# A hybrid attention layer: six output tiles, the sample's sums a step later, pools that wait by tile, and a scale per token

## The chip, the cores and the metric

The kernel runs on one core of one Trainium2 chip. The metric is device time in microseconds (us) for one execution. The core has a matrix engine (PE), a vector engine (DVE), a scalar engine (ACT), a general engine (POOL) and a queue (SP) that issues all of this kernel's transfers, which 16 DMA engines carry out. Every engine takes its instructions in the order of its own queue.

## The reference

One layer of a decoder. It is computed for a prompt of 2048 tokens and for a sample of 8 sequences with 8 new tokens each, whose keys and values of the last 2048 positions lie in a cache. Cut to what matters here:

```
h = rmsnorm(x, norm_w)
q, k, v, qb, kb, vb, g_lr, gate_a, gate_b = split(h @ w_in)
q, k = rope(rmsnorm(q)), rope(rmsnorm(k))                # 8 heads x 64
o_a = mixture of 3 dilated windows (128,1) (512,4) (2048,16), weighted by their softmax denominators
o_b = gated linear attention(qb, kb, vb, g_lr, state)    # 4 heads, key 64, value 128
o_b = rmsnorm(o_b, gla_norm_w)
mixed = concat(o_a * silu(gate_a), o_b * silu(gate_b))
y = x + mixed @ w_out
```

It returns y of prompt and sample, the prompt's keys and values, the sample's new keys and values, and the states of the linear attention.

## The kernel before

Tokens go in 16 tiles of 128, called t, and the sample's 64 tokens as one tile "s". Large products use pairs of f16 tiles, a high and a low part (three products for each), and each operand is scaled by a power of two ahead of it. Intermediate results go through DRAM (q_d, k_d, o1_d to o3_d, gw_d, ga_d, ob_d and others).

The stages, in the order in which the code writes them:

1. Weights v, q and k are loaded; `first(m)` projects v, q and k for four tiles at a time (m = 0 to 3). Between its steps the main loop adds `3 * rate` to `credit` and, for every whole unit of it, advances a software pipeline of attention work by one step (`pump`). Units of branches 1 and 2 are queued after each m. A unit writes its outputs, maxima and denominators into a tile `o` of the pool `op` (L367, four tiles) and stores it to o1_d or o2_d. L414 on DVE masks the scores and takes their maxima into `o`; ACT exponentiates (L417); PE transposes (L424); ACT, and DVE or POOL, split the result into two f16 parts (L386, L387, or L389 to L391); PE multiplies by the values (L439); DVE adds two parts into `o` (L456).
2. Beside it run 64 steps of `sample_scores` (one or two after each projection of m = 2 and 3, the rest in stage 3). A step loads a row of queries (qt, L929), keys k3 (L931) and, every second time, keys k2 (L934), and calls `dot` twice: POOL multiplies into the one tile pr (L919), DVE sums it at once (L920). The tiles k3 and qt come from two buffers each, k2 and pr from one.
3. `rest("qkb")` projects the keys and queries of the linear attention, woven with what is left of the attention, with branch 3 (16 residues; its tile o3 is from the pool b3, two tiles, stored at L894), with the loading of weights g and vb (`load_w`) and with the remaining dots. `weave` runs several generators in turns: next is the one whose share of its announced number of steps is least, and one that must wait yields WAIT.
4. The attention's pools are closed; the pools gl, gt and gst take their place. g and vb are projected, woven with the linear attention (`gla_all`, GLA) and the loading of weights gb; then gb, woven with GLA and the loading of the output weights o0 and o1, until gb and the weights are done. `silu` keeps the maxima of its results by row, in one column of gmax["a"] or gmax["b"] per call.
5. The pools of the projections (wr, zp, hp, hps, on the right side of SBUF) are closed, and cb and cb1 take their place. The maxima are reduced over all columns and, by `spread_max` (a transpose on PE, a reduction, a product with ones), over all partitions. This gives one scale smx for all tokens, and from it smxa and inv_o.
6. `prompt_out`: `combine(t)` loads the three branches (L1421), ob, gw and ga (L1424 to L1428), mixes them, scales by smx and smxa, splits into two f16 parts (L1365, L1366) and transposes them by a DMA (L1368); `finish` multiplies by the output weights (L1404, 48 products a tile), rescales by inv_o and adds x (L1411), and stores y (L1415). combine runs one tile ahead. Woven with it is `sample_attention` on the pools ssk and ss1, on the left side: it loads value tiles (L1664, eight buffers) and multiplies them one step at a time (L1639).

A pool that is opened on the bytes of closed pools has all its tiles wait, by default, for every user of those pools. The engines' queues are not in the order of the code throughout: in the trace, value tiles of stage 6 are loaded while gb is still projected.

Of the kernel before, what the change touches and what calls it, by code (L numbers as in the profile page):

```python
# [18 lines left out]
P = 128  # L19
# [33 lines left out]
def tile_hymba(ctx: ExitStack, tc: tile.TileContext, A: dict):  # L53
# [293 lines left out]
    with ExitStack() as c1:  # L347
# [8 lines left out]
        def right(stack, name, bufs):  # L356
            return stack.enter_context(tc.tile_pool(name=name, bufs=bufs, side="right"))
# [9 lines left out]
        op = c_att.enter_context(tc.tile_pool(name="op", bufs=4))  # L367
# [549 lines left out]
        def dot(out, kt, qt, tag):  # L917
            pr = sk.tile([P, 512], F32, name=f"pr_{tag}", tag="pr", bufs=1)
            POOL.tensor_tensor(pr[:], kt, qt, ALU.mult)  # L919
            DVE.tensor_reduce(  # L920
                out, pr[:].rearrange("p (u k d) -> p u k d", u=2, k=4), AX.X, ALU.add
            )

        def sample_scores(b, t):
# [12 lines left out]
            dot(out[:, 1], k3[:], qt[:], f"3_{b}_{t}")  # L937
            dot(out[:, 0], sk_state["k2"][:], qt[:], f"2_{b}_{t}")
            if t == 7:
                SP.dma_start(sc_d[b * P : (b + 1) * P, :], sc[:].rearrange("p g c -> p (g c)"))  # L940
# [157 lines left out]
        for m in range(4):  # L1098
# [9 lines left out]
            rate = 0.62  # L1108
            if m == 1:
                for b in range(8):  # L1110
                    for t in (0, 4, 1, 5, 2, 6, 3, 7):
                        side.append(lambda b=b, t=t: sample_scores(b, t))
        c_first.close()
# [35 lines left out]
        gl = c_gla.enter_context(tc.tile_pool(name="gl", bufs=2))  # L1149
        gt = c_gla.enter_context(tc.tile_pool(name="gt", bufs=1))  # L1150
        gst = c_gla.enter_context(tc.tile_pool(name="gst", bufs=1))
# [83 lines left out]
        def sample_gla():  # L1235
            c_sg = ExitStack()
            g1 = c_sg.enter_context(tc.tile_pool(name="sg1", bufs=1))
# [77 lines left out]
        for names, loads, n_ in ((("g", "vb"), ("gb",), 45), (("gb",), ("o0", "o1"), 0)):  # L1315
            host = [rest(*names), sum(steps(name) for name in names)]
            fetch = [chain(*(load_w(x) for x in loads)), len(loads) * (2 * KT + 1)]
            left = weave(host, gla_all, fetch, until=[host, fetch])
            gla_all = left[0] if left else [iter(()), 1]
            gla_all[1] = n_ or 100  # L1320


        c_in.close()
        cb = right(c1, "cb", 2)
        cb1 = right(c1, "cb1", 1)
# [3 lines left out]
        bound = sm.tile([P, 2], F32, name="bound", tag="bound", bufs=1)  # L1329
        for i, n_ in enumerate("ab"):  # L1330
            g = sm.tile([P, 1], F32, name=f"gm_{n_}", tag="gm")
            DVE.tensor_reduce(g[:], gmax[n_][:], AX.X, ALU.max)
            DVE.tensor_copy(bound[:, i : i + 1], spread_max(g[:], f"g{n_}"))
        DVE.scalar_tensor_tensor(
            bound[:, 0:1], bound[:, 0:1], 2048.0, powers["v"][:], ALU.mult, ALU.mult
        )
        g = sm.tile([P, 1], F32, name="gm_n", tag="gm")
        DVE.tensor_reduce(g[:], gnw[:], AX.X, ALU.max, apply_absolute_value=True)
        DVE.scalar_tensor_tensor(
            bound[:, 1:2], bound[:, 1:2], 11.4, g[:], ALU.mult, ALU.mult  # L1340
        )
        p2 = sm.tile([P, 1], F32, name="p2", tag="p2", bufs=1)
        DVE.tensor_tensor(p2[:], bound[:, 0:1], bound[:, 1:2], ALU.max)
        power(p2[:], p2[:])
        smx = kp.tile([P, 1], F32, name="smx")
        DVE.reciprocal(smx[:], p2[:])
        DVE.tensor_scalar(smx[:], smx[:], M_SCALE, None, ALU.mult)

        smxa = kp.tile([P, 1], F32, name="smxa")
        DVE.tensor_scalar(  # L1350
            smxa[:], smx[:], powers["v"][:], 1.0 / (P_SCALE * W_SCALE * H_SCALE * V_SCALE),
            ALU.mult, ALU.mult,
        )
        inv_o = []
        for nh in range(2):
            t = kp.tile([P, 1], F32, name=f"inv_o{nh}")
            DVE.tensor_scalar(
                t[:], loaded[f"o{nh}"][1][:], p2[:], 1.0 / M_SCALE, ALU.mult, ALU.mult
            )
            inv_o.append(t)  # L1360
# [29 lines left out]
        def finish(tag, n, mixed_parts, xsrc, ydst):  # L1390
# [8 lines left out]
            for nh in range(2):  # L1399
                cs = slice(512 * nh, 512 * nh + 512)  # L1400
                w_, inv = loaded[f"o{nh}"][0], inv_o[nh]
# [15 lines left out]
        def combine(t):  # L1417
            rows = slice(t * P, (t + 1) * P)
            oc = cb.tile([P, 3, NH, 66], F32, name=f"oc_{t}", tag="oc")
            for g, src in enumerate((o1_d, o2_d, o3_d)):  # L1420
# [24 lines left out]
                w[:], w[:], smxa[:], mn[:].unsqueeze(1).to_broadcast([P, 3, NH]),  # L1445
                ALU.mult, ALU.mult,
            )
            DVE.scalar_tensor_tensor(mix[:, 512:], ob[:], smx[:], gw[:], ALU.mult, ALU.mult)
# [15 lines left out]
        def sample_out():  # L1464
# [15 lines left out]
            for i in range(2):  # L1480
                a_, b_ = ts_[2 * i : 2 * i + 2]
                DVE.scalar_tensor_tensor(
                    mix[:NS, 512 * i : 512 * i + 512], a_[:NS], smx[:NS], b_[:NS],
                    ALU.mult, ALU.mult,
                )
            yield from finish("s", NS, sample_parts(mix), x_s, y_s)

        def prompt_out():
            while 0 not in mixed:
                yield WAIT  # L1490
            mixes = {0: combine(0)}
            for t in range(NT):
                while t + 1 < NT and t + 1 not in mixed:
                    yield WAIT
                if t + 1 < NT:
                    mixes[t + 1] = combine(t + 1)
# [289 lines left out]
```

## Time and profile before

| what | us |
|---|---|
| median of 3 runs | 1474.63 (1474.44 to 1477.34) |
| the profiled execution | 1477.99 |
| its span, first to last instruction | 1476.2 |
| PE busy | 1282.4 |
| DVE busy | 980.5 |
| ACT busy | 831.8 |
| POOL busy | 622.6 |
| 16 DMA engines, mean busy share | 0.74 |

How to read the lines that the prediction shows. A line of a wait reads "engine tile line <- what ended the wait: us in total, times, longest". A line of the timeline reads "start, length, engine, line, operation, output <- inputs, shapes, count", and in square brackets the engine's idle time ahead of it and what ended it. A line of a table by windows reads "from:to length, busy us (instructions) of PE, weight load, DVE, ACT and POOL, then the granted TensorE clock, the DMA share and GB/s"; where one line or engine alone is asked for, only its columns are there. A line of the table of transfers gives the count, the size of one and the median us from issue to landing.

### The profile page before, as it was taken

What the parts mean: (1) busy time and instruction counts of PE and PEld (TensorE: products, weight loads), DVE (VectorE), ACT (ScalarE), POOL (GpSimd) and SP (SyncE); (2) the same over time, 40 slices, a digit from 0 to 9 for tenths busy, and PEclk for the clock granted to TensorE, in tenths of its full rate; (3) what the DMA queues carried; (4) which work ended last, traced back from release to release, by engine and by line L of the source; (5) the groups of instructions that cost most, each with busy time, mean ns of one, the idle gap of its engine ahead of it and who ended that gap; (6) DMA issues with size and microseconds to landing.
All of it is one profiled execution on the core that took longest, in us unless ns stands there. A gap on an engine that the chain in (4) does not pass through costs nothing. (4 is left out here: it accounts for less than half of the span.)

```text
span 1476.2 us, 25889 instructions
## 1 busy us (share of the span) xinstructions
PE 1282.4 (87%) x8628; PEld 733.9 (50%) x8628; DVE 980.5 (66%) x2393; ACT 831.8 (56%) x2263; POOL 622.6 (42%) x564
## 2 busy tenths in 40 slices
PE   4796899998989889995869999889989969999878
PEld 1343455554555555664546755667545433433323
DVE  6476687777878946665554466798887567534453
ACT  6645688676667666865657754777786621100100
POOL 0043333566766544664341376545562334212221
PEclk9998899999999899997989999989999969999989
DMA  9877668587886799879998444243135689999993
GB/s 266 262 179 182 181 176 218 152 227 218 202 212 183 224 239 277 284 207 233 268 226 203 131 127 125 93 137 115 60 115 173 201 267 292 302 318 314 288 299 122
DMA packets 321240, 306.29 MB, mean 207 GB/s; under 512 B 192258, under 2 KB 223059, under 8 KB 321107
## 3 DMA queue, kind: packets, MB, share of 16 engines
q1 hardware_dynamic: 321106, 304.64, 73.7%
q8 instruction: 68, 1.11, 0.3%
q14 instruction: 66, 0.53, 0.1%
HBM read 183.19 MB, written 79.43 MB: 178 GB/s over the span
## 5 line engine op out<-in xcount | busy, mean ns | idle before, releaser
L919 POOL TENSOR_TENSOR pr<-k,qb 128x512 f32<-128x512 f32 x128 | 173.8, 1358 | 185.2 <-DVE sck L920 88.7
L1050 PEld LDWEIGHTS <-hr 128*128 128x128 f16 x1824 | 175.8, 99 | 139.6 <-issue 19.6
L417 ACT ACTIVATE p<-p,o 128x256 f32<-128x256 f32 (+1 forms) x384 | 173.0, 453 | 93.8 <-DVE o L414 85.8
L1050 PEld LDWEIGHTS <-hl 128*128 128x128 f16 x1248 | 124.4, 102 | 148.9 <-issue 35.6
L1404 PE MATMUL Y<-w_o,mh 128*128 128x512 f16 x768 | 180.3, 388 | 17.4 <-DMA mh<-mt 12.1
L414 DVE CUSTOM_DVE_ANT_0 p<-s,m3w,scl_s 128x256 f32<-128x256 f32 (+1 forms) x384 | 143.7, 419 | 52.3 <-DMA o_d<-o 36.1
L391 POOL TENSOR_TENSOR pt<-p,pt 128x512 f16<-128x512 f32 (+1 forms) x80 | 96.3, 1204 | 156.2 <-ACT pt L390 120.6
L920 DVE TENSOR_REDUCE sck<-pr 128x8 f32<-128x512 f32 x128 | 87.0, 679 | 89.5 <-POOL pr L919 89.4
L424 PE MATMUL t<-ident,p 128*128 128x128 f32 x600 | 117.1, 292 | 30.7 <-ACT p L417 28.3
L439 PE MATMUL O<-v,pt 128*128 128x128 f16 x1200 | 115.6, 223 | 31.0 <-POOL pt L391 19.1
L1404 PEld LDWEIGHTS <-mh 128*128 128x128 f16 x768 | 73.4, 99 | 120.1 <-issue 29.4
L1050 PE MATMUL acc_v<-w_v,hl 128*128 128x512 f16 x384 | 103.7, 411 | 19.1 <-ACT zs_k L646 9.3
L406 PE MATMUL s<-kk,qq 128*128 128x256 f16 (+1 forms) x512 | 108.4, 326 | 12.6 <-DVE o L414 10.9
L439 PEld LDWEIGHTS <-pt 128*128 128x128 f16 x1200 | 85.7, 100 | 67.3 <-POOL pt L391 25.3
L1452 POOL TENSOR_TENSOR tc<-oc,w 128x512 f32<-128x512 f32 x32 | 44.2, 1400 | 158.6 <-DVE w L1444 131.6
L424 PEld LDWEIGHTS t<-ident,p 128*128 128x128 f32 x600 | 74.1, 148 | 59.2 <-ACT p L417 44.8
L1050 PE MATMUL acc_g<-w_g,hr 128*128 128x272 f16 (+1 forms) x768 | 100.1, 277 | 1.5 <-ACT vbs L720 1.5
L1050 PE MATMUL acc_q<-w_q,hl 128*128 128x512 f16 x384 | 96.3, 388 | 1.8 <-ACT zs_q L646 1.4
L1050 PE MATMUL acc_k<-w_k,hl 128*128 128x512 f16 x384 | 95.3, 383 | 0.5 <-DVE vp L733 0.5
L1050 PE MATMUL acc_vb<-w_vb,hr 128*128 128x512 f16 x384 | 90.4, 383 | 4.1 <-DVE so_g L620 4.1
L1365 ACT ACTIVATE mt<-mix 128x1024 f16<-128x1024 f32 x16 | 16.9, 1056 | 130.5 <-DVE mix L1459 100.2
L1050 PE MATMUL acc_gb<-w_gb,hr 128*128 128x512 f16 x384 | 88.7, 386 | 0.0
(529 smaller groups left out, 2588.3 us busy)
## 6 DMA issues: line engine op xcount, KB each, us to landing
k<-in_cache_k_win SPq DMA_DIRECT2D x104, 256.0 KB, 4.9
sv<-in_cache_v_win SPq DMA_DIRECT2D x104, 256.0 KB, 5.5
hr<-h_d SPq DMA_DIRECT2D x44, 512.0 KB, 4.8
qb<-q_d SPq DMA_DIRECT2D x64, 256.0 KB, 4.9
oc<-o_d SPq DMA_DIRECT2D x48, 264.0 KB, 5.8
o_d<-o SPq DMA_DIRECT2D x64, 132.0 KB, 4.2
x<-in_x_prompt SPq DMA_DIRECT2D x16, 512.0 KB, 5.7
h_d<-hl SPq DMA_DIRECT2D x16, 512.0 KB, 4.7
```

The lines of the kernel that those rows point to most:

```text
L391: POOL.tensor_tensor(l, f, h, ALU.subtract)
L406: PE.matmul(s_ps[:, i * w : (i + 1) * w], q, k, start=(n == 0), stop=(n == len(prods) - 1),)
L414: DVE.tensor_tensor_reduce(s[:, sl], s_ps[:, sl], mask, neg, BIG, ALU.add, ALU.min, nmf(i))
L417: ACT.activation(s[:, sl], s[:, sl], AF.Exp, bias=nmf(i), scale=-1.0, accum_out=denf(i))
L424: PE.transpose(p_ps[:, i * P : (i + 1) * P], t["s"][:, i * P : (i + 1) * P], ident[:])
L439: PE.matmul(o_, t["pt"][:, c, (i * nb + b) * P : (i * nb + b + 1) * P], vf(i, b), start=(n == 0), stop=(n == 2 * nb - 1),)
L919: POOL.tensor_tensor(pr[:], kt, qt, ALU.mult)
L920: DVE.tensor_reduce(out, pr[:].rearrange("p (u k d) -> p u k d", u=2, k=4), AX.X, ALU.add)
L1050: PE.matmul(z, a_[:, k, :], w[:, p_, k, cols], start=(k == 0 and i == 0), stop=(k == KT - 1 and i == 2),)
L1365: ACT.activation(mt[:, 0], mix[:], AF.Copy)
L1404: PE.matmul(Y[:], a_[:, k, :], w_[:, part, k, :512], start=(i == 0), stop=(i == len(prods) - 1),)
L1452: eng.tensor_tensor(t_[:], oc[:, g, :, 0:64], w[:, g].unsqueeze(2).to_broadcast([P, NH, HD]), ALU.mult,)
```

## The change

- Every pool on the right side, the pools of the linear attention, and cb, cb1, ssk and ss1 are opened with `reuse_waits="tile"`: a tile then waits only for the users of earlier tiles on its own bytes.
- `op` has six tiles in place of four.
- `dot` and pr are gone. A step of `sample_scores` first sums the products of the step before (`dot_sums`), then multiplies into k3 and into qt, in place. The last sums are a step of their own.
- After m = 0 the credit is set to -14; before it went on from 0. The rate of 0.62 stays.
- GLA runs to its end inside the projection of gb, its final state is stored there, and its pools are closed; cb and cb1 are opened on the left side, in their place. What is left of gb and of the output weights then runs on, woven with `first_mixes`, which calls `scales` for the sample and tokens' tiles 0 to 10 and `combine` for tiles 0 and 1, as soon as gb's tiles 11 and 12 are projected.
- The scale is one per token: row p and column of p2, smx and smxa belong to one token, and the reductions over all columns and both `spread_max` go away. inv_o has 17 columns.
- ssk and ss1 are opened on the right side, after the pools of the projections are closed.
- `sample_pair` loads value tiles of two steps and then multiplies both; it has fewer steps, and is announced as 4 x 16 in place of 4 x 24.

The diff, cut to its core:

```diff
-            return stack.enter_context(tc.tile_pool(name=name, bufs=bufs, side="right"))
+            return stack.enter_context(
+                tc.tile_pool(name=name, bufs=bufs, side="right", reuse_waits="tile")
+            )
...
-        op = c_att.enter_context(tc.tile_pool(name="op", bufs=4))
+        op = c_att.enter_context(tc.tile_pool(name="op", bufs=6))
...
-        def dot(out, kt, qt, tag):
-            pr = sk.tile([P, 512], F32, name=f"pr_{tag}", tag="pr", bufs=1)
-            POOL.tensor_tensor(pr[:], kt, qt, ALU.mult)
-            DVE.tensor_reduce(
-                out, pr[:].rearrange("p (u k d) -> p u k d", u=2, k=4), AX.X, ALU.add
-            )
+        def dot_sums():
+            prods, last = sk_state.pop("sums", ((), None))
+            for out, pr in prods:
+                DVE.tensor_reduce(
+                    out, pr[:].rearrange("p (u k d) -> p u k d", u=2, k=4), AX.X, ALU.add
+                )
+            if last:
+                b, sc = last
+                SP.dma_start(sc_d[b * P : (b + 1) * P, :], sc[:].rearrange("p g c -> p (g c)"))
...
-            dot(out[:, 1], k3[:], qt[:], f"3_{b}_{t}")
-            dot(out[:, 0], sk_state["k2"][:], qt[:], f"2_{b}_{t}")
-            if t == 7:
-                SP.dma_start(sc_d[b * P : (b + 1) * P, :], sc[:].rearrange("p g c -> p (g c)"))
+            dot_sums()
+            POOL.tensor_tensor(k3[:], k3[:], qt[:], ALU.mult)
+            POOL.tensor_tensor(qt[:], sk_state["k2"][:], qt[:], ALU.mult)
+            sk_state["sums"] = (
+                [(out[:, 1], k3), (out[:, 0], qt)], (b, sc) if t == 7 else None
+            )
...
-            rate = 0.62
+            if m == 0:
+                rate, credit = 0.62, -14.0
...
-        for names, loads, n_ in ((("g", "vb"), ("gb",), 45), (("gb",), ("o0", "o1"), 0)):
-            host = [rest(*names), sum(steps(name) for name in names)]
-            fetch = [chain(*(load_w(x) for x in loads)), len(loads) * (2 * KT + 1)]
-            left = weave(host, gla_all, fetch, until=[host, fetch])
-            gla_all = left[0] if left else [iter(()), 1]
-            gla_all[1] = n_ or 100
-        c_in.close()
-        cb = right(c1, "cb", 2)
-        cb1 = right(c1, "cb1", 1)
+        host = [rest("g", "vb"), steps("g") + steps("vb")]
+        fetch = [load_w("gb"), 2 * KT + 1]
+        left = weave(host, gla_all, fetch, until=[host, fetch])
+        gla_all = left[0] if left else [iter(()), 1]
+        gla_all[1] = 45
+        host = [rest("gb"), steps("gb")]
+        fetch = [chain(load_w("o0"), load_w("o1")), 4 * KT + 2]
+        left = weave(host, gla_all, fetch, until=[gla_all])
+        host, fetch = left
...
+        c_gla.close()
+        cb = c1.enter_context(tc.tile_pool(name="cb", bufs=2, reuse_waits="tile"))
+        cb1 = c1.enter_context(tc.tile_pool(name="cb1", bufs=1, reuse_waits="tile"))
...
+        def scales(i0, i1):
+            c = slice(i0, i1)
+            DVE.tensor_reduce(
+                p2[:, c], gmax["a"][:, 2 * i0 : 2 * i1].rearrange("p (t two) -> p t two", two=2),
+                AX.X, ALU.max,
+            )
+            DVE.tensor_scalar(p2[:, c], p2[:, c], powers["v"][:], 2048.0, ALU.mult, ALU.mult)
+            DVE.tensor_scalar(bnd[:, c], gmax["b"][:, c], gn[:], 11.4, ALU.mult, ALU.mult)
+            DVE.tensor_tensor(p2[:, c], p2[:, c], bnd[:, c], ALU.max)
+            power(p2[:, c], p2[:, c])
+            DVE.reciprocal(smx[:, c], p2[:, c])
+            DVE.tensor_scalar(smx[:, c], smx[:, c], M_SCALE, None, ALU.mult)
...
+        def first_mixes():
+            for t in range(2):
+                while ("gb", 11 + t) not in done:
+                    yield WAIT
+                if t == 0:
+                    scales(0, 12)
+                mixes[t] = combine(t)
+                yield
...
+        weave(host, fetch, [first_mixes(), 2])
+        c_in.close()
+        scales(12, NT + 1)
...
-        ssk = c1.enter_context(tc.tile_pool(name="sk2", bufs=2))
-        ss1 = c1.enter_context(tc.tile_pool(name="ss1", bufs=1))
+        ssk = right(c1, "sk2", 2)
+        ss1 = right(c1, "ss1", 1)
...
-                values(ps, vs_, i + 1)
-                yield
+                held.append((ps, vs_, i + 1))
+                if i % 2 == 0:
+                    while held:
+                        values(*held.pop(0))
+                    yield
...
-        weave(out, [sample_attention(), 4 * 24])
+        weave(out, [sample_attention(), 4 * 16])
```

85 lines of the change are left out of this document (34 added, 51 removed).

## The prediction

> **What bounds the kernel now.** I read the busy table and the slices first, then busy time by stage, then the waits of the stages in which TensorE (PE) idles, then the timeline of three holes and of the hand-over from the last projection to the output.
>
> ```profile
> span 1476.2 us, 25889 instructions
> PE 1282.4 (87%) x8628; PEld 733.9 (50%) x8628; DVE 980.5 (66%) x2393; ACT 831.8 (56%) x2263; POOL 622.6 (42%) x564
> ...
> 90.00:200.00 110.00, 90.01 (x511) 47.77 (x509) 76.41 (x186) 66.59 (x182) 34.50 (x36) 0.91 0.71 182
> 200.00:640.00 440.00, 403.15 (x2666) 241.61 (x2665) 330.35 (x800) 311.87 (x860) 253.05 (x188) 0.96 0.80 217
> 640.00:840.00 200.00, 160.35 (x1322) 114.33 (x1321) 110.22 (x426) 132.45 (x455) 68.62 (x59) 0.91 0.86 217
> 840.00:1100.00 260.00, 234.42 (x1939) 154.71 (x1938) 204.20 (x396) 178.96 (x468) 161.05 (x188) 0.96 0.37 110
> 1100.00:1184.00 84.00, 83.92 (x509) 44.44 (x507) 52.58 (x127) 56.08 (x126) 23.82 (x24) 1.00 0.55 176
> 1184.00:1220.00 36.00, 20.88 (x147) 10.28 (x147) 24.02 (x71) 7.12 (x15) 13.47 (x11) 0.58 0.91 288
> 1220.00:1440.00 220.00, 198.67 (x1162) 81.52 (x1161) 115.53 (x246) 22.11 (x44) 52.99 (x41) 0.95 1.01 302
> ```
>
> After the window's length the columns are PE, weight load, DVE, ACT, POOL, granted clock, DMA share, GB/s. PE is the bound, and its work is nearly untouched by the change, so a gain has to come out of its idle time: 1476.2 - 1282.4 = 193.8 us in all. By stage (length less busy) it idles 20.0 us at the start of the attention, 36.9 in its middle (200 to 640), 39.7 in its last branch (640 to 840), 25.6 under the gated linear attention (GLA), 0.1 under the projection gb, 15.1 at the hand-over, 21.3 in the output stage. In the output stage the DMA share is 1.01: it is tied to transfers as much as to PE.
>
> **The sample's products and the output tiles (200 to 640).**
>
> ```profile
> POOL pr L919 <- DVE sck L920: 61.0, 43, 3.9
> DVE sck L920 <- POOL pr L919: 57.6, 32, 7.3
> ...
> DVE p L414 <- DMA o_d<-o: 11.7, 6, 2.5
> ...
> PE O L439 <- POOL pt L391: 11.8, 8, 4.2
> PE s L406 <- DVE o L414: 9.9, 7, 3.4
> PE t L424 <- ACT p L417: 6.0, 7, 2.5
> ```
>
> Each of the 128 dots writes one tile pr, of which there is one: POOL multiplies, DVE sums at once, POOL waits for the sum. Both queues are in order, so the attention's L414 on DVE and L391 on POOL stand behind these waits. The change writes the products over k3 and qt and sums them a step later: same instructions, no pr, and DVE finds its operand ready. Six tiles o in place of four give the store two more units to land before L414 writes to the tile again; their 2 x 1 KB per partition take what pr's 2 KB leaves. The two causes are 57.6 + 11.7 = 69.3 of DVE's 440 - 330.35 = 109.7 idle us, 63%. PE's three waits on the attention's chain are 11.8 + 9.9 + 6.0 = 27.7 us. If they fell with DVE's idle time, 0.63 x 27.7 = 17.5 us would go. But ACT, 311.87 us busy, and POOL lie on that chain too, and what DVE doesn't stall for it partly queues for. Bounds 0 and 17.5; I take half, **9 us**.
>
> **The last branch (640 to 840).**
>
> ```profile
> DVE sck L920 <- POOL pr L919: 31.7, 16, 6.5
> ...
> DVE p L414 <- DMA o_d<-o: 24.4, 10, 5.0
> ...
> PE t L424 <- ACT p L417: 20.8, 6, 7.7
> ...
> 675.29 1.26 POOL L919 TENSOR_TENSOR pr<-k,qb 128x512 f32<-128x512 f32 x1 [5.79 <-DMA k<-in_cache_k_win]
> 676.58 0.69 DVE L920 TENSOR_REDUCE sck<-pr 128x8 f32<-128x512 f32 x1 [5.44 <-POOL pr L919]
> 677.71 0.93 PE L439 MATMUL O<-v,pt 128*128 128x128 f16 x7 [5.35 <-POOL pt L391]
> ...
> 685.36 0.35 DVE L414 CUSTOM_DVE_ANT_0 p<-s,m3w,scl_s 128x128 f32<-128x128 f32 x1 [2.92 <-DMA o_d<-o]
> 686.35 0.48 PE L424 MATMUL t<-ident,p 128*128 128x128 f32 x1 [7.71 <-ACT p L417]
> 748.17 0.35 DVE L414 CUSTOM_DVE_ANT_0 p<-s,m3w,scl_s 128x128 f32<-128x128 f32 x1 [5.03 <-DMA o_d<-o]
> 749.11 0.48 PE L424 MATMUL t<-ident,p 128*128 128x128 f32 x1 [7.62 <-ACT p L417]
> ```
>
> At 670 a late key load holds POOL, POOL holds the sum, the sum holds DVE for 5.44 us, and PE loses 5.35. A later sum takes DVE out of that chain, though POOL still stands at the product with L391 behind it. The other two holes, 7.71 and 7.62 us, end on the store of an o tile of 128x128 scores. That is branch 3, whose o3 comes from the pool b3 with two tiles, not from op: the six tiles do nothing there. So of 20.8 us on ACT p only 20.8 - 15.3 = 5.5 are open, and with the 5.35 at most 10.9 us. The lower bound is 0, since the stage's DMA share is 0.86. Half again: **5 us**.
>
> **Start of the attention.** The credit of -14 at 3 x 0.62 per step puts the first unit 8 projection steps later. PE idles 20.0 us there, from 90 to 200, in waits on ACT and DVE that the first units sharpen; 14 steps of attention then run later, in a stage that is fuller. From -3 to 5; I take **2**.
>
> **Pools that wait by tile.** Their first tiles no longer wait for all users of the bytes' former pools. For GLA that could fill a part of the 25.6 us idle there, but PE's idle time under GLA is spread through it and DVE is at 204.20 of 260. From 0 to 4; I take **1**.
>
> **The hand-over (1184 to 1220).**
>
> ```profile
> 1163.79 1.65 SPq L1664 DMA_DIRECT2D sv<-in_cache_v_win  x3
> ...
> 1192.56 1.28 SPq L1421 DMA_DIRECT2D oc<-o_d  x3
> ...
> 1219.62 17.67 PE L1404 MATMUL Y<-w_o,mh 128*128 128x512 f16 x72 [0.74 <-issue]
> ...
> 1245.01 5.35 PE L1404 MATMUL Y<-w_o,mh 128*128 128x512 f16 x24
> ...
> 1160.00:1170.00 10.00, 10.00 (x49) 4.58 (x48) 3.41 (x9) 4.97 (x10) 3.42 (x4) 1.00 0.98 303
> 1170.00:1180.00 10.00, 10.00 (x49) 4.54 (x48) 7.67 (x15) 7.45 (x14) 2.93 (x2) 1.00 0.51 183
> 1180.00:1190.00 10.00, 5.42 (x27) 3.00 (x25) 6.14 (x19) 3.96 (x6) 4.20 (x4) 0.80 0.20 68
> ...
> oc<-o_d SPq DMA_DIRECT2D x48, 264.0 KB, 5.8
> ```
>
> Today one scale for all tokens needs the maximum over all of gb, two spreads over the partitions, and the pools cb and cb1 on the bytes of the projections. So the first load oc goes out at 1192.56 and the first Y starts at 1219.62; meanwhile PE has only the sample's work, at a clock of 0.58. A scale per token needs that token's own maxima: tiles 0 and 1 are mixed under gb's last tiles, where PE is busy 10 of 10 us and DVE 7.67 at most, in the rows of 10 us below 1180, and Y can start at about 1185. Both spreads go (four small matmuls). On PE the gain is the 15.1 idle us plus the lost clock. For Y that is 17.67 - 3 x 5.35 = 1.6 us; for the sample's value products I compare two windows of L1639 alone:
>
> ```profile
> 1184.00:1220.00 36.00, 10.09 (x64) 0.58 0.91 288
> 1220.00:1440.00 220.00, 40.41 (x384) 0.95 1.01 302
> ```
>
> 158 against 105 ns each, 64 x 53 = 3.4 us. Together 20.1 us, if nothing else bounds. Transfers do: with the share at 1.01 the output stage only ends sooner by bytes moved before it. Tiles 0 and 1 bring 2 x (3 x 264 + 3 x 256) KB = 3.2 MB forward, 10.6 us at 302 GB/s. The sample's pools move to the side that the projections free last, so its first eight value tiles, now loaded around 1165 at 303 GB/s, go behind: 2.1 MB, 6.9 us. What remains is 3.7 us plus the trough from 1180 to 1190, filled: 0.80 x 10 = 8 us. That is 11.7; bounds 3.7 and 20.1, I take **12 us**.
>
> The Trainium skill (DMA: Bandwidth & Descriptors, Specifications) puts a core's share of HBM at about 358 GB/s. By it the output stage at 302 would have room, and the sum would take 20 rather than 12 us here. The share of 1.01 in the row above speaks for 12.
>
> Two loads per value step, and fewer steps, change no bytes in a stage tied to bytes: 0, from -3 to 3. The scales' DVE instructions grow from 1 to 17 columns: 0, beside instructions of 0.7 us.
>
> **Sum.** 9 + 5 + 2 + 1 + 12 = 29 us. The profiled execution took 1477.99 us, 1.8 around its span, and lies 3.4 above the median 1474.63. 1477.99 - 29 = 1449; against the median **1446 us**.
>
> **Rivals.**
> *A. A wait in the queue of transfers (slower).* A buffer qt or k3 now comes free at the sum, a step later, not at the product:
>
> ```profile
> SPq L931 <- POOL pr L919: 33.6, 21, 3.8
> SPq L929 <- POOL pr L919: 27.4, 14, 5.1
> ...
> SPq L934 <- POOL pr L919: 7.7, 9, 1.7
> ...
> PE O L439 <- DMA v<-vp_d: 0.8, 1, 0.8
> ...
> k<-in_cache_k_win SPq DMA_DIRECT2D x104, 256.0 KB, 4.9
> ```
>
> At odd tiles two steps are issued together: 2 x 3 x 2 = 12 pairs. The second load then waits for a sum just issued, behind DVE's backlog, and holds the loads of v, hr and queries behind it in SP's queue. A load takes 4.9 us to land; POOL's product, with L391 behind it, waits as long. Twelve times 4.9 is 59 us; half of it passed to PE eats the 14 gained in the attention and 15 more: 1474.6 + 29 - 15 = 1489. It decides from some six pairs on. For it: SP waits 68.7 us on products already, with L934. Against it: PE waited 0.8 us for v, so loads run ahead.
> *B. The attention gives nothing*, since ACT and POOL take DVE's place: 1474.6 - 15 = 1460.
> *C. The output stage has room*: its transfers could run closer together than at 302 GB/s, PE sets its end, and the waits elsewhere pass on in full: 17.5 + 10.9 + 5 + 4 + 20.1 = 57.5, 1417. Against it: the share of 1.01. The rule above is for it.
> *D. Waits by tile don't reach the sample's pools*: they start only after 1190, and the hand-over gives 3.7: 1454.
>
> **Chances.** Forecast 0.43, B 0.15, C 0.12, D 0.10, A 0.14, and 0.06 that gains and A cancel. A measurement tells 0.2%, 3 us, from no change. So faster 0.79, same 0.06, slower 0.15. The range takes in D, B and most of C, and stops short of A: 1420 to 1480; the forecast's own is 1434 to 1456.
>
> **What would show it.** The waits of sck on pr and of pr on sck under 30 us in all; o_d waits left only where o3 is stored; the hole near 670 gone and those of o3 still there. The first Y within 5 us of gb's last matmul, a clock near 1 across it, DMA share over 0.8 from 1160 on. Wrong: SP waits on sck L920 that exceed 70 us, or an output stage no shorter counted from gb's end.

## The result, and the profile after

| what | us |
|---|---|
| median of 8 runs after | 1482.40 (1478.37 to 1485.88) |
| median of 8 runs before, on the same chip | 1474.54 (1469.47 to 1477.64) |
| ratio | 1.0047, 95% interval 1.0026 to 1.0069 |
| the profiled execution after, and its span | 1482.47, 1480.7 |

The changed kernel is slower by 0.5%, where 1446 us was forecast. Between the two profiled executions the span grew by 1480.7 - 1476.2 = 4.5 us.

The head of the page after:

```profile
span 1480.7 us, 25918 instructions
PE 1284.8 (87%) x8622; PEld 731.3 (49%) x8622; DVE 997.9 (67%) x2396; ACT 828.4 (56%) x2263; POOL 624.8 (42%) x564
```

PE's work stayed (1282.4 before). The same stages as before, by windows, with the same columns:

```profile
90.00:200.00 110.00, 89.05 (x505) 47.34 (x503) 77.76 (x184) 65.95 (x181) 36.00 (x37) 0.92 0.70 186
200.00:640.00 440.00, 386.34 (x2475) 229.42 (x2473) 340.44 (x770) 290.59 (x798) 256.13 (x192) 0.94 0.79 218
640.00:840.00 200.00, 176.51 (x1427) 121.77 (x1426) 111.32 (x436) 142.47 (x483) 61.00 (x51) 0.96 0.85 207
840.00:1100.00 260.00, 238.69 (x1983) 159.49 (x1981) 196.06 (x397) 181.76 (x481) 154.77 (x182) 0.97 0.38 115
1100.00:1184.00 84.00, 81.14 (x529) 44.64 (x528) 65.84 (x161) 59.36 (x144) 31.93 (x30) 1.00 0.57 188
1184.00:1220.00 36.00, 23.26 (x98) 9.73 (x96) 35.00 (x70) 8.91 (x15) 23.46 (x16) 0.81 0.83 244
1220.00:1440.00 220.00, 196.25 (x1215) 78.03 (x1214) 102.74 (x231) 22.62 (x48) 46.05 (x38) 0.95 1.02 305
```

Length less PE's busy time, stage by stage: the middle of the attention lost 440 - 386.34 = 53.7 us, where it had lost 36.9; the last branch lost 23.5 where it had lost 39.7. What one gave the other took. DVE is now busy 35.00 of 36 us at the hand-over (24.02 before), and the output stage still runs at a DMA share of 1.02.

Where the end moved is best read at marks: the last sum of the dots, the last products of k and of gb, and the end. First the kernel before, by tiles (durations in ns, least, median and most; then the first and the last start):

```profile
L920 DVE TENSOR_REDUCE sck<-pr x128: 664/680/689, 273.6 to 773.9; 128x8 f32<-128x512 f32 x128
L1050 PE MATMUL acc_k<-w_k,hl x384: 376/379/631, 86.9 to 483.2; 128*128 128x512 f16 x192
L1050 PE MATMUL acc_gb<-w_gb,hr x384: 378/379/635, 1061.8 to 1183.0; 128*128 128x512 f16 x192
L1664 SPq DMA_DIRECT2D sv<-in_cache_v_win x104: 327/382/1134, 1162.3 to 1423.7; - x104
```

Then the kernel after:

```profile
L923 DVE TENSOR_REDUCE sck<-qb x64: 664/682/689, 275.2 to 738.1; 128x8 f32<-128x512 f32 x64
L1058 PE MATMUL acc_k<-w_k,hl x384: 376/379/631, 86.0 to 497.8; 128*128 128x512 f16 x192
L1058 PE MATMUL acc_gb<-w_gb,hr x384: 378/379/634, 1057.8 to 1189.1; 128*128 128x512 f16 x192
L1418 PE MATMUL Y<-w_o,mh x768: 376/379/634, 1199.6 to 1475.4; 128*128 128x512 f16 x192
L1687 SPq DMA_DIRECT2D sv<-in_cache_v_win x104: 327/382/1552, 1215.9 to 1429.2; - x104
```

The dots end 35.8 us sooner, the projection of k 14.6 us later, and gb 1189.1 - 1183.0 = 6.1 us later. Gb's first product started 1061.8 - 1057.8 = 4.0 us sooner, so it is under gb itself that the changed kernel falls behind: 131.3 us from its first product to its last, where it was 121.2. From there to the end it was 1476.2 - 1183.0 = 293.2 us and is 1480.7 - 1189.1 = 291.6. The first Y came 20.0 us earlier (1199.6 against 1219.6, 10.5 us behind gb's last product), as the change was to bring about, and almost nothing of that arrived at the end. The first value load of the sample went from 1162.3 to 1215.9.

The waits of the attention's middle (200 to 640) after, first the engines':

```profile
DVE sck L923 <- POOL k L944: 46.0, 26, 3.9
POOL k L944 <- DMA qb<-q_d: 44.5, 15, 7.2
POOL qb L945 <- DMA k<-in_cache_k_win: 22.1, 8, 9.0
...
DVE sck L923 <- POOL qb L945: 18.4, 16, 3.2
...
POOL k L944 <- DMA k<-in_cache_k_win: 16.0, 3, 8.9
```

then those of SP's queue in the same window:

```profile
SPq L937 <- DVE sck L923: 33.7, 18, 4.5
...
SPq L935 <- DVE sck L923: 12.0, 15, 3.0
```

and of the last branch (640 to 840), the wait for the store of an output tile:

```profile
DVE p L416 <- DMA o_d<-o: 33.5, 11, 4.7
```

DVE still waits for POOL at the sums, 46.0 + 18.4 = 64.4 us where it was 57.6. POOL hardly waits for a sum any more (5.2 us, where it was 61.0) but for loads: 44.5 + 22.1 + 16.0 = 82.6 us, where it was 34.4 + 11.8 = 46.2. The loads (L935, L937) wait in SP's queue for the sum that frees their buffer, 45.7 us in all; before, the same loads had stood there 61.0 us for the products. The six tiles did what was expected of them: the waits on the store of o, 11.7 us between 200 and 640 before, are no longer among that window's, and those of the last branch, on o3, are there still.

At the hand-over after, the timeline of SP's queue shows the sample's loads behind the last store of the projections:

```profile
1209.56 0.33 SPq L719 DMA_DIRECT2D gw_d<-gw  x1
...
1211.47 0.38 SPq L1542 DMA_DIRECT2D hm<-in_c_hm  x1
...
1215.88 1.27 SPq L1687 DMA_DIRECT2D sv<-in_cache_v_win  x3
```

and PE's timeline shows what it waits for between gb and the output:

```profile
1173.77 15.71 PE L1058 MATMUL acc_gb<-w_gb,hr 128*128 128x512 f16 x72
1199.64 13.37 PE L1418 MATMUL Y<-w_o,mh 128*128 128x512 f16 x48 [10.16 <-DMA mh<-mt]
```

PE has nothing to do for 10.16 us: the mixed tile comes late, and the sample's work, which filled this stretch before, cannot start.

### The profile page after: what moved, and what is told of

Same layout as the page of the kernel before. It is cut to its first block, busy times and chain, and to the rows that moved or that the text cites. A ratio compares the mean times of both kernels' runs of the same rounds, so it can differ in the third digit from the quotient of the medians.

```text
span 1480.7 us, 25918 instructions
## 1 busy us (share of the span) xinstructions
PE 1284.8 (87%) x8622; PEld 731.3 (49%) x8622; DVE 997.9 (67%) x2396; ACT 828.4 (56%) x2263; POOL 624.8 (42%) x564
## 5 line engine op out<-in xcount | busy, mean ns | idle before, releaser
L1418 PE MATMUL Y<-w_o,mh 128*128 128x512 f16 x768 | 181.3, 386 | 16.8 <-DMA mh<-mt 13.7
L944 POOL TENSOR_TENSOR k<-k,qb 128x512 f32<-128x512 f32 x64 | 83.6, 1307 | 116.9 <-DMA qb<-q_d 55.4
L426 PE MATMUL t<-ident,p 128*128 128x128 f32 x600 | 120.6, 293 | 12.9 <-ACT p L419 10.9
L1058 PE MATMUL acc_v<-w_v,hl 128*128 128x512 f16 x384 | 97.5, 399 | 19.7 <-ACT zs_k L648 8.5
L945 POOL TENSOR_TENSOR qb<-k,qb 128x512 f32<-128x512 f32 x64 | 85.3, 1334 | 46.2 <-DMA k<-in_cache_k_win 31.7
L210 ACT ACTIVATE E<-D_e 128x256 f32<-128x256 f32 (+1 forms) x168 | 67.5, 411 | 30.0 <-DVE ks L217 18.3
```

What stands on the lines that cost most here:

```text
L210: ACT.activation(E[rows, i, :n], D[rows, half], AF.Exp, scale=1.0 / 16.0)
L426: PE.transpose(p_ps[:, i * P : (i + 1) * P], t["s"][:, i * P : (i + 1) * P], ident[:])
L944: POOL.tensor_tensor(k3[:], k3[:], qt[:], ALU.mult)
L945: POOL.tensor_tensor(qt[:], sk_state["k2"][:], qt[:], ALU.mult)
L1058: PE.matmul(z, a_[:, k, :], w[:, p_, k, cols], start=(k == 0 and i == 0), stop=(k == KT - 1 and i == 2),)
L1418: PE.matmul(Y[:], a_[:, k, :], w_[:, part, k, :512], start=(i == 0), stop=(i == len(prods) - 1),)
```

## The experiments

18 kernels, each timed beside the kernel before on the same chip (medians before: 1473.3 to 1475.1). Base is the kernel that was edited.

| label | base and edit | us | ratio, 95% interval |
|---|---|---|---|
| e1_dots_only | before, new dots | 1495.47 | 1.016 (1.0138 to 1.0182) |
| e2_tail_only | before, new output part | 1480.05 | 1.0048 (1.0024 to 1.0071) |
| e3_waits_only | before, pools wait by tile | 1472.08 | 0.9991 (0.9967 to 1.0015) |
| e4_after_old_dots | after, old dots, 5 tiles o | 1487.25 | 1.01 (1.0078 to 1.0122) |
| e5_dots_three | room, new dots, three k3 and qt | 1475.45 | 1.002 (1.0 to 1.0041) |
| e6_dots_own | room, sums later, own product tiles | 1488.26 | 1.01 (1.0068 to 1.0133) |
| e7_credit_only | before, credit -14 | 1485.58 | 1.0082 (1.0049 to 1.0115) |
| e8_o5_only | room, 5 tiles o | 1462.38 | 0.9934 (0.9909 to 0.9959) |
| e9_room_only | before, room alone | 1486.86 | 1.0073 (1.0044 to 1.0102) |
| e10_dots_o6 | before, new dots, 6 tiles o | 1477.56 | 1.0029 (1.0007 to 1.0051) |
| e11_after_no_credit | after, credit as before | 1482.80 | 1.0053 (1.0033 to 1.0073) |
| e12_tail_left | e2, sample's pools left | 1458.41 | 0.988 (0.9845 to 0.9915) |
| e13_after_left | after, sample's pools left | 1471.66 | 0.9975 (0.9953 to 0.9997) |
| e14_tail_ss1_right | e2, only ssk left | 1468.31 | 0.9962 (0.9938 to 0.9985) |
| e15_o5_tail_left | e8 with the output part of e12 | 1478.71 | 1.0022 (1.0001 to 1.0044) |
| e16_after_op4 | after, 4 tiles o | 1486.97 | 1.0079 (1.0052 to 1.0107) |
| e17_after_k3_three | e16, three k3 | 1475.74 | 1.0016 (0.9992 to 1.0041) |
| e18_tail_left_again | e12, unchanged | 1455.38 | 0.9894 (0.9861 to 0.9926) |

### The parts alone

e1 takes the new `dot_sums` and the products in place into the kernel before, with four tiles o:

```diff
+            dot_sums()
+            POOL.tensor_tensor(k3[:], k3[:], qt[:], ALU.mult)
+            POOL.tensor_tensor(qt[:], sk_state["k2"][:], qt[:], ALU.mult)
```

> The kernel before with the new dots alone (products in place, sums a step later; pools, credit, four o tiles and the output part as before). Theory 1, loads wait for sums: a buffer of qt or k3 comes free a step later, so loads are issued later, POOL waits for them and DVE for POOL; the projections of q and k end 10 to 20 us later than before (last acc_k near 495 instead of 483.2), and the time is 1480 to 1495. Rival 2, the dots are neutral and the attention's loss comes from the pools, the credit or the o tiles: within 3 us of before.

1495.47 us, a loss of 22, about what theory 1 named. That the ring alone costs it is not shown, since the queues' order changes with the edit too. Between 200 and 640 DVE's waits at the sums were 49.2 and 17.0 us, as in the changed kernel, and 13.6 us at the store of o. The last product of the keys started at 506.0 (483.2 before).

e2 takes all from `gla_all` on, so scales, combine, the pools' sides and sample_pair, into the kernel before, without waits by tile:

```diff
-        ssk = c1.enter_context(tc.tile_pool(name="sk2", bufs=2))
-        ss1 = c1.enter_context(tc.tile_pool(name="ss1", bufs=1))
+        ssk = right(c1, "sk2", 2)
+        ss1 = right(c1, "ss1", 1)
```

> The kernel before with the output part alone (GLA ended inside gb, two tiles mixed under gb, scale per token, sample pools on the right side, two value steps at once), without waits by tile. Theory 3, transfers bound the output stage and the sample's loads come 50 us later than before, so the earlier first Y is given back: first Y under 1200, time within 4 us of before. Rival 4, the hand-over pays as forecast and other parts lose it: 1458 to 1466.

1480.05 us, a loss of 7 where the forecast had a gain of 12. This comparison is clean up to gb: the first 6625 of PE's 8622 products stand in the order of before, and the next one lies in gb. The first Y started at 1186.1, 0.2 us after gb's last product at 1185.9, and from there to the end it took 1480.2 - 1185.9 = 294.3 us.

e3 gives the pools on the right, gl, gt, gst and sg1 `reuse_waits="tile"` and nothing else:

```diff
-            return stack.enter_context(tc.tile_pool(name=name, bufs=bufs, side="right"))
+            return stack.enter_context(
+                tc.tile_pool(name=name, bufs=bufs, side="right", reuse_waits="tile")
+            )
```

> The kernel before with waits by tile alone (right side pools and those of the linear attention). Theory 5, the linear attention starts sooner after the attention, from which the changed kernel regained some 25 us between the attention's end and gb's start: 1455 to 1468. Rival 6, that regain is work that was only shifted, and waits by tile change nothing: 1471 to 1478.

No effect that can be told: 0.9991 (0.9967 to 1.0015). The order of every queue is that of before; only the waits differ.

e7 sets the credit alone:

```diff
+            if m == 0:
+                rate, credit = 0.62, -14.0
```

> The kernel before with the credit of -14 alone. Theory 8, the changed kernel with old dots lost some 11 us between the projections' end and gb to attention that was put off by the credit: the attention ends 5 to 12 us later (last O of it 842 to 849), time 1478 to 1486. Rival 9, it gains the 2 us of the prediction: 1470 to 1475.

A loss of 12 us, and PE idle 110 - 88.45 = 21.6 us at the attention's start (20.0 before). So the start did not gain, and the attention's last product of the values came at 843.0 (836.7 before), as theory 8 had it. But e11, the changed kernel without the credit,

```diff
-                rate, credit = 0.62, -14.0
+            rate = 0.62
```

> The changed kernel without the credit of -14. Theory 8, the credit costs the changed kernel what it costs the kernel before, 12 us: 1466 to 1474. Rival 16, the credit helps the new dots, whose first loads it lets run ahead: 1482 or more.

took 1482.80 us, against 1482.40 with it: in the changed kernel the credit is worth nothing.

### The dots and the output tiles

e4 gives the changed kernel its old dots back, with five tiles o, since pr leaves no room for six:

```diff
-            dot_sums()
+            dot(out[:, 1], k3[:], qt[:], f"3_{b}_{t}")
+            dot(out[:, 0], sk_state["k2"][:], qt[:], f"2_{b}_{t}")
```

> The changed kernel with the old dots back (one product tile, summed at once) and five o tiles, which is what fits. Theory 1: the attention's loss goes, last acc_k back near 483, time 1460 to 1470. Rival 2: time stays at 1478 to 1486.

1487.25 us. The projections' end came back (last product of the keys at 482.1, 497.8 in the changed kernel), and at gb's last product (1196.1) the kernel was 7.0 us behind the changed one. Shortening the middle of the attention did not shorten the kernel.

e10 is e1 with six tiles o:

```diff
-        op = c_att.enter_context(tc.tile_pool(name="op", bufs=4))
+        op = c_att.enter_context(tc.tile_pool(name="op", bufs=6))
```

> The kernel before with the new dots and six o tiles, which together use the same room as before. Theory 14, the parts add: 22 from the dots less 11 or a little more from the o tiles, 1478 to 1486. Rival 15, the o tiles take away what the dots cost, since both act on the same queue: 1462 to 1474.

1477.56, so 17.9 us better than e1; the 13.6 us at the store of o between 200 and 640 are gone. Both parts together cost 1.0029. In the changed kernel the same edit backwards,

> The changed kernel with four o tiles. Theory 21, in the changed kernel the six o tiles are worth what they are beside the new dots alone, 18 us (1495.47 against 1477.56): 1494 to 1506. Rival 22, they are worth the 3 to 6 us of the prediction: 1484 to 1489.

is worth only 1486.97 - 1482.40 = 4.6 us.

For e5, e6, e8 and e15 bytes were needed, so two small constants are made later, in a pool of the linear attention. That edit, called room, runs alone in e9:

```diff
-    ident8 = cp.tile([P, P], F32, name="ident8")
-    DVE.tensor_scalar(ident8[:], ident[:], 0.125, None, ALU.mult)
...
-        gnw = const1("gnw", [P, P], A["gla_norm_w"].to_broadcast([P, P]))
...
+        gnw = const2("gnw", [P, P], A["gla_norm_w"].to_broadcast([P, P]))
+        ident64 = gst.tile([P, 64], F32, name="ident64")
```

> The kernel before with nothing but the room that three runs used (two constants of the linear attention made later, two small tiles gone): the control for the third buffer, the products of their own and the five o tiles. Theory 12, the room is neutral: 1470 to 1477, first sum near 273.6. Rival 13, the run with the third buffer began its sums 10 us sooner (263 against 273.6) because of the room: 1462 to 1468, and each of the three runs must be read against this one.

It cost 12 us, though it moves one load and a few DVE instructions of the start. It also has another order of the queues: matched by tile and line of code, at most 934 of the 1149 transfers in SP's queue stand in their old order, where in e3 all 1149 do. So 12 us can come with another order alone, and what the other edits of this section show in sums of that size is not proof of their mechanism.

e5, a third buffer for k3 and qt beside the new dots, and e6, sums a step later out of two product tiles of their own, so that no buffer of k3 or qt is held for them (the second cut is against the products in place):

```diff
-            k3 = sk.tile([P, 512], F32, name=f"k3_{b}_{t}", tag="k3")
+            k3 = sk.tile([P, 512], F32, name=f"k3_{b}_{t}", tag="k3", bufs=3)
```

> The kernel before with the new dots and a third buffer for qt and k3, so that a load need not wait for the sum of the step just issued (room from constants of the linear attention that are made later). Theory 1, the ring from sum to load to product costs the 22 us of the dots alone: time 1468 to 1480, waits of POOL's products on the loads of qt and k3 under 40 us. Rival 7, the sums in pairs, in front of the attention's own DVE work, cost it: time stays above 1486.

```diff
-            POOL.tensor_tensor(k3[:], k3[:], qt[:], ALU.mult)
+            POOL.tensor_tensor(pr3[:], k3[:], qt[:], ALU.mult)
```

> The kernel before with sums a step later, but products into two tiles of their own (k3 and qt come free at the product, as before). Theory 1: time 1468 to 1480. Rival 7: above 1486, since the sums stand where they stand in the dots alone.

1475.45 and 1488.26 us, against 1486.86 for room alone and 1495.47 for e1. The time of e5 is in the range of theory 1, but not its waits: POOL's waits on the loads were to fall under 40 us and are, between 200 and 640,

```profile
POOL qb L937 <- DMA k<-in_cache_k_win: 53.9, 13, 8.8
...
POOL k L936 <- DMA qb<-q_d: 39.5, 18, 5.4
```

So its gain is not shown to be the ring's either. e6 has no ring, and POOL waits 30.4 us for the sums in that window (61.9 in room), yet its time is that of room: less waiting for the sum bought nothing there.

> The kernel before with five o tiles (room as in the run with the third buffer). Theory 10, the store of o is off the path that sets the end: waits of L414 on the store fall under 4 us from 200 to 640, time within 3 us of before. Rival 11, it pays as forecast, some 3 to 6 us: 1467 to 1471.

1462.38: five tiles o (`bufs=5`) beat the kernel before by 0.9934, and room by 24 us (20 by the two ratios), more than all waits on the store of o between 200 and 640 (11.7 us before, 16.4 in room). Waits alone cannot have given that; part of it goes with another order of the queues.

The ring was tried once more in the changed kernel with four tiles o (e16), with a third buffer for k3 alone; a third for qt as well was not tried, since there is no room for it.

> The changed kernel with four tiles o (1486.97 us) and a third buffer for the keys k3 of the sample's products. Theory 20 (ring): a key load of the changed kernel waits for the sum of two products before, SP stood 33.7 us there between 200 and 640, and that holds the product and what stands behind it; with a third buffer SP's waits on sums at the load of k3 fall under 10 us and the time falls by 10 us or more, to 1477 or less. Rival 21: the wait in SP's queue is covered, loads run ahead anyway, and the time stays within 4 us, 1483 to 1491. Rival 22: the waits fall but the queues are planned in another order and the time moves by as much as that has moved others, either way up to 12 us; a slower time would show it.

11.2 us faster than e16, as theory 20 had it, yet not by its mechanism. SP's waits at the load of k3 in e16, between 200 and 640:

```profile
SPq L937 <- DVE sck L923: 27.7, 17, 5.1
```

and in e17:

```profile
SPq L937 <- DVE sck L923: 32.3, 21, 3.8
```

They did not fall. That speaks against the ring's wait as the price and for the order of the queues (rival 22, which however had the waits falling): at most 822 of the 1149 transfers in SP's queue stand in the order of e16.

### The side of the sample's pools

e12 is e2 with ssk and ss1 on the left, behind cb1; the attention's order is the same in both, and the queues part in gb (SP's behind the first 851 of its 1153 instructions, at 1144 us):

```diff
-        ssk = right(c1, "sk2", 2)
-        ss1 = right(c1, "ss1", 1)
+        ssk = c1.enter_context(tc.tile_pool(name="sk2", bufs=2))
+        ss1 = c1.enter_context(tc.tile_pool(name="ss1", bufs=1))
```

> The kernel before with the output part of the change, but with the sample's pools on the left side, in the linear attention's place, so that its loads need not wait for the projections' pools. Theory 3, the late sample loads (1213 in place of 1162) give the earlier first Y back: the first loads of value tiles come before 1180 and the time falls to 1462 to 1472. Rival 17, DVE, busy 9.3 to 10 of 10 us from 1160 to 1210 in the run with the output part alone, is what gives it back: 1476 to 1484, loads early or not.

1458.41, and once more, unchanged,

> The fastest kernel so far once more, unchanged, to see whether its 16.7 us below the kernel before stand: 1455 to 1462 if they do; within 5 us of the kernel before if they were chance.

1455.38: 21.6 and 24.7 us below e2, and 0.988 and 0.9894 of the kernel before. It is the fastest of all. One of the six runs of e12 took 4283.33 us, which nothing on record explains; the other five and all six of e18 lie between 1451.70 and 1464.21. Rival 17 is out with it as the main price: DVE is as full in e12, 35.98 of 40 us from 1180 to 1220. SP's queue in e2, on the right side:

```profile
1206.62 0.54 SPq L717 DMA_DIRECT2D gw_d<-gw  x1
...
1209.38 0.42 SPq L1531 DMA_DIRECT2D hm<-in_c_hm  x1
...
1213.28 5.06 SPq L1676 DMA_DIRECT2D sv<-in_cache_v_win  x8
```

and in e12, on the left:

```profile
1142.24 1.06 SPq L1676 DMA_DIRECT2D sv<-in_cache_v_win  x2
...
1144.30 3.77 SPq L1676 DMA_DIRECT2D sv<-in_cache_v_win  x5
...
1182.65 0.38 SPq L1531 DMA_DIRECT2D hm<-in_c_hm  x1
```

On the right the pools lie on bytes that the projections' last tiles use, up to the store of gw at 1206.62; hm comes 2.76 us behind it and the values after that. The order of SP's queue puts them there: its wait just ahead of hm took 0.03 us. On the left the bytes were free by 1142, and hm goes out 21.8 us ahead of the last store of gw (1204.45). The holes of PE in e2 at that place:

```profile
1178.07 8.22 PE L1050 MATMUL acc_gb<-w_gb,hr 128*128 128x512 f16 x24 [7.60 <-DVE so_gb L620]
1186.12 5.34 PE L1407 MATMUL Y<-w_o,mh 128*128 128x512 f16 x24
1192.68 5.35 PE L1407 MATMUL Y<-w_o,mh 128*128 128x512 f16 x24 [1.21 <-DVE so_gb L620]
1206.58 13.02 PE L1407 MATMUL Y<-w_o,mh 128*128 128x512 f16 x49 [8.54 <-DVE xr L1414]
```

and in e12, with the sample's products in them:

```profile
1173.17 6.62 PE L1050 MATMUL acc_gb<-w_gb,hr 128*128 128x512 f16 x24 [3.39 <-DVE so_gb L620]
...
1185.78 7.16 PE L1407 MATMUL Y<-w_o,mh 128*128 128x512 f16 x24
...
1202.33 0.64 PE L1650 MATMUL OS<-sv,P 128*32 128x256 f32 x8
```

The transfers tell where the time went. The windows of e2 from its first gb to the end:

```profile
1057.00:1186.00 129.00, 118.43 (x762) 64.19 (x761) 104.00 (x230) 90.21 (x219) 55.25 (x56) 0.95 0.56 183
1186.00:1220.00 34.00, 24.24 (x106) 10.28 (x105) 29.07 (x60) 7.32 (x12) 24.52 (x19) 0.85 0.86 252
1220.00:1440.00 220.00, 194.19 (x1205) 80.84 (x1204) 97.32 (x218) 21.46 (x46) 42.75 (x33) 0.93 1.01 286
1440.00:1480.00 40.00, 29.38 (x144) 11.28 (x141) 8.57 (x14) 0.77 (x2) 0.00 (x0) 0.88 0.35 113
```

and those of e12:

```profile
1057.00:1180.00 123.00, 116.43 (x751) 63.18 (x748) 93.91 (x212) 87.47 (x211) 49.62 (x51) 0.97 0.59 198
1180.00:1220.00 40.00, 33.36 (x211) 15.57 (x212) 35.98 (x84) 10.94 (x21) 24.87 (x20) 0.91 0.92 263
1220.00:1410.00 190.00, 171.94 (x1056) 69.29 (x1054) 89.95 (x195) 18.14 (x37) 42.04 (x32) 0.96 1.03 310
1410.00:1452.00 42.00, 37.02 (x176) 16.07 (x174) 16.45 (x29) 2.05 (x4) 3.82 (x3) 1.00 0.49 140
```

Both move the same bytes: length by GB/s, summed, is 99.6 MB in e2 and 99.7 MB in e12. Length by DMA share, summed, is 338 us of 423 in e2 and 326 us of 395 in e12. So of the 28 us between these two executions 16 are time in which the transfers stood idle, and 12 are transfers that took longer for the same bytes (286 against 310 GB/s at a share of 1). Why the rate differs no view shows.

> The changed kernel with the sample's pools on the left side, in the linear attention's place, all else as changed. Theory 3, their side costs in the changed kernel what it costs beside the old attention, 22 us (1480.05 against 1458.41): 1455 to 1465, value tiles loaded before 1185. Rival 18, waits by tile and the later attention take that cost over: 1474 or more.

The same edit in the changed kernel gave 1482.40 - 1471.66 = 10.7 us, half of it. 1471.66 us lies below the range of rival 18 and above that of theory 3. From gb's last product (1182.1) to the end (1464.0) it took 281.9 us, against 291.6: the gain is where it should be, though the first Y started at 1204.1, later than in the changed kernel. How early the first Y starts is thus not what sets the end. That gb's first product came 8.2 us sooner (1049.6 against 1057.8) is not the edit's: up to gb, PE's products stand in the same order in both. So far apart can two executions of the same attention be.

e14 keeps ss1, with hm and the scores, on the right and brings ssk, with the value tiles, to the left:

```diff
-        ssk = right(c1, "sk2", 2)
+        ssk = c1.enter_context(tc.tile_pool(name="sk2", bufs=2))
```

> The kernel before with the output part of the change, the value tiles and keys of the sample (ssk) on the left side, its small tiles (ss1) on the right: the first eight value tiles can be loaded under gb, but no score, mask or product of the sample can start before the projections' last store. Theory 19, what counts are the bytes that move before the output stage is tied to transfers: 1458 to 1468. Rival 20, what counts is the sample's work on PE and DVE in the hand-over: 1474 to 1482.

1468.31 us, just above the range of theory 19 (1458 to 1468): early value loads alone (from 1148.9 on) bring 11.7 of the 21.6 to 24.7 us. The rest goes with ss1, whose hm again comes behind the last store of gw (1215.24 after 1211.34); that it is the later start of the scores that costs it is argued, not shown.

> Five o tiles (with the room for them), old dots, no credit, and the output part with the sample's pools on the left side: the parts that gained. If gains add, 1462 less 17: 1442 to 1452. If the order in which the queues are laid out decides more than the parts, anywhere from 1450 to 1475.

1478.71 us, though each half alone had been 11 and 16 to 18 us faster than before. The halves do not add. The attention kept its half: its last product of the values started at 815.8, as in e8 (815.7; 836.7 before). From gb's last product (1169.7) to the end (1474.4) it took 304.7 us, against 272.9 in e12: the output part lost more than it had gained. Its value loads started at 1191.4 and not at 1142.2, though the pools lie on the left here too. From 1150 to 1200 SP's queue stood 18.3 us for POOL's gw, and the value loads are placed behind the loads oc of three tiles; PE had nothing to do for 16.64 us ahead of the scores. So the left side allows early loads and does not bring them by itself. Why they were planned later is open.

## Why the prediction was wrong

**The hand-over, 12 us: the step that failed.** The mechanism came in its first half: the first Y 20.0 us earlier in the changed kernel, though 10.5 us behind gb and not within 5, and in e2 0.2 us behind gb. The step "The sample's pools move to the side that the projections free last, so its first eight value tiles ... go behind: 2.1 MB, 6.9 us" was mis-sized. The side costs 21.6 and 24.7 us (e12 and e18 against e2) and 10.7 in the changed kernel (e13). The prediction counted the bytes of eight tiles; it left out that every first tile of those pools, hm and the scores' operands among them, stands behind the last store of the projections, and that PE then has none of the sample's work for its holes. With 6.9 replaced by 21.6 to 24.7, the term of 11.7 becomes a loss of 3 to 6 us; e2 measured a loss of 7. With the 10.7 of the changed kernel it would still be a gain of 8, so there the side is not all. That store came late, moreover, because of the change itself: before, the last one went out at

```profile
1190.47 0.32 SPq L717 DMA_DIRECT2D gw_d<-gw  x1
```

7.5 us behind gb's last product, and after, at 1209.56, 20.5 us behind it. The row of 10 us under gb's end after reads

```profile
1180.00:1190.00 10.00, 9.48 (x44) 4.12 (x42) 10.00 (x16) 4.10 (x7) 4.53 (x3) 1.00 1.03 387
```

with DVE at 10.00 where it was 6.14. The prediction had placed the mixing beside "DVE 7.67 at most" and priced it at nothing; DVE is full, and gb's evictions and the stores of gw stand behind it (the hole of 7.60 us on so_gb in e2). From gb's first product to its end PE idles 10.1 us after and 10.6 in e2, where it idled 5.5 before: some 5 us that the sum had at nothing. The list had "an output stage no shorter counted from gb's end" as the sign of an error: 293.2 before, 291.6 after, 294.3 in e2.

**The dots and the output tiles, 9 us.** "DVE finds its operand ready" did not come true: 64.4 us of waits where under 30 were expected. The sum frees the buffer, the buffer lets the load go, the load lets POOL multiply, and the next sum needs that product: the two-buffer ring of rival A. Its waits in SP's queue, 33.7 + 12.0 = 45.7 us, stay under the 70 named for it, and under the 61.0 that the same loads stood there before. Rival A's own sum is wrong besides: by its words the 59 us, halved, eat all 29 us of gains, which gives 1474.6, and 1489 sets only 15 of them against it. PE's idle time in that stage rose by 16.8 us. What share of this is the ring's is open: e17 gained 11.2 us without shortening its waits, and e5 gained without POOL's waits on loads falling.

**The last branch, 5 us.** Right in kind and too small: PE's idle time fell by 16.2 us. The hole near 670 is gone (from 640 to 840 no hole of PE is longer than 3.87 us), the waits on o3 remain, 33.5 us. But that is not a gain by itself: the dots now end at 738.1 where they ended at 773.9, so work was moved from this stage into the one before. The two terms together, forecast 14, came to -0.6 us of PE's idle time, and e10 to a loss of 0.3% (0.07 to 0.51).

**The credit, 2 us, and the waits by tile, 1 us.** Nothing of either: e11 and e3. The start of the attention idled 110 - 89.05 = 21.0 us, 20.0 before.

**The output stage.** Its tie to transfers stands: a share of 1.02 at 305 GB/s after. The Trainium skill (DMA: Bandwidth & Descriptors, Specifications) gives a core about 358 GB/s of HBM, by which rival C expected room; no run raised the long row above 310 (e12), so the traces leave the bound of the prediction standing. Short rows do reach more, 387 in the fence above, but GB/s there counts all that the engines move, not HBM alone.

**The sum.** By their ratios to before, e10 (+4.3 us), e2 (+7.1), e3 (-1.3) and the credit as e11 has it (0) make 10 us; the changed kernel's ratio is 6.9 us (3.8 to 10.2). That they nearly agree is in part luck, for with the credit as e7 has it (12 us) they make 22. The price that was too small in the sum was that of the pools' side, and the gains set against it in the attention did not exist.

## What to carry to other kernels

When the first work of a stage is brought forward, look at the bytes on which the work beside it will lie: two pools opened on the side that is freed last moved their first value load by 50 us and cost 10 to 25 us, more than the early mixing had gained. Before a sum is put off a step, follow the buffer that now waits for it round to its next load, for one wait may only change its name. Where a planner orders the queues, run an edit that should change nothing, and don't read a mechanism out of differences that it alone can make.

## What the runs showed beside this

Another order of the queues can come with sums like those of the edits. Room (e9), which leaves the attention's code as it was, moved the time by 12 us of 1475, and with it at most 934 of 1149 transfers in SP's queue kept their order; e3, which leaves every queue's order alone, moved it by nothing. Gains found alone (e8: 11 us, e12: 16 to 18) were gone when joined (e15: a loss of 3 to 4). PE's queue is equal up to gb in before and e2, in e2 and e12, e14, e18, in e13 and the changed kernel, and in e8 and e15; in the comparisons of the dots, the tiles o in the attention and the credit it is not. And the same queue has its own spread: in the profiled executions gb's first product, ahead of which the queues are the same, started between 1056.4 and 1063.0 in e2, e12, e14 and e18.

Transfers can be busy all the time and still differ in what they move: at shares of 1.01 to 1.03 the output stage ran at 286 GB/s in e2, 302 before, 305 after and 310 in e12.
